# Whole-tile instructions in a split GELU-multiply kernel, with the first and last tiles cut smaller

## The chip, the cores and the metric

The kernel runs on one core of a Trainium2 chip. The metric is device time in microseconds (us) of one execution. The kernel before takes 471.6 us. The names in the profile: ACT is the scalar engine, which computes the GELUs; DVE is the vector engine, which multiplies; SP computes nothing and only issues transfers; the 16 DMA engines move the data.

## The reference

```python
def reference(x):                      # x: (32, 512, 2048) float32
    half_dim = x.shape[-1] // 2
    x1, x2 = x[..., :half_dim], x[..., half_dim:]
    gelu_x1 = 0.5 * x1 * (1 + erf(x1 / np.sqrt(2)))
    return (gelu_x1 * x2).astype(np.float32)
```

134.2 MB come in and 67.1 MB go out, with one GELU and one multiply per output element.

## The kernel before

The 16,384 rows are cut in 16 tiles of 128 partitions x 8 rows. A tile is 8.39 MB of input and 4.19 MB of output. There are two input and two output buffers. Loads are issued from SP's queue and stores from ACT's, except that the last two tiles are stored from SP's.

```python
R, STEP = 8, 4
xpool = ...tile_pool(name="xpool", bufs=2)
opool = ...tile_pool(name="opool", bufs=2)
...
ahead = [load(0), load(1)]                       # nc.sync.dma_start
for i in range(n_tiles):
    x_tile = ahead.pop(0)
    o_tile = opool.tile(...)
    last = i == n_tiles - 1
    for r in range(0, R, STEP):                  # two halves of 4 rows
        rows = slice(r, r + STEP)
        nc.scalar.activation(out=x_tile[:, rows, :half], in_=x_tile[:, rows, :half], func=GELU)
        nc.vector.tensor_mul(out=o_tile[:, rows, :], in0=..., in1=x_tile[:, rows, half:])
        if last:
            store(nc.sync, i, o_tile, rows)
    if not last:
        store(nc.sync if i == n_tiles - 2 else nc.scalar, i, o_tile, slice(0, R))
    if i + 2 < n_tiles:
        ahead.append(load(i + 2))
```

The build, which turns the source into one queue of instructions per engine, orders each queue itself.

## Time and profile before

| | before |
|---|---|
| time, median | 471.6 us |
| profiled span | 469.7 us |
| DVE / ACT busy | 140.2 / 115.2 us |
| moved over the span | 201.3 MB, 429 GB/s |
| period of a tile | 29.0 us at 434 GB/s |

How to read it: compute is busy less than a third of the time (DVE 30%, ACT 25%), and the DMA engines are busy throughout (a share of 1.00 in each stretch of a tile). The prediction below shows the lines. One view that it did not use is the order of ACT's queue. The timeline around tiles 4 and 5 of the kernel before shows it (start, duration, engine, line, operation; in brackets, how long the engine stood idle before and what ended that; ACTq is ACT's sequencer, which issues the DMA):

```profile
131.71 7.12 ACT L54 ACTIVATE x_tile<-x_tile 128x4096 f32<-128x4096 f32 x2 [22.10 <-DMA x_tile<-in_x_dram]
135.36 8.76 DVE L57 TENSOR_TENSOR o_tile<-x_tile 128x4096 f32<-128x4096 f32 x2 [20.47 <-ACT x_tile L54]
144.15 0.36 ACTq L45 DMA_DIRECT2D out_dram<-o_tile  x1
160.50 7.12 ACT L54 ACTIVATE x_tile<-x_tile 128x4096 f32<-128x4096 f32 x2 [21.67 <-DMA x_tile<-in_x_dram]
```

The multiplies of tile 4 end at 144.12 and its store goes out at 144.15, 16.4 us ahead of the next tile's GELU.

### The profile page before, as it was taken

The numbers are of one execution on the slowest core, as the hardware profiler recorded it, in microseconds if no ns is written. First come the engines' busy times: TensorE is split into PE (matmuls) and PEld (weight loads), VectorE is DVE, ScalarE is ACT, GpSimd is POOL, SyncE is SP. The second block draws the span as 40 slices with busy tenths as digits, with TensorE's granted clock in tenths as the row PEclk, the third lists the DMA queues.
The fourth block names the chain that finished last, engine by engine and source line by source line (L and its number), as shares of the span: only waits on it lengthen the run. The fifth ranks groups of instructions, "written<-read, shape, count | busy, mean of one in ns | idle before, by whom it ended". The sixth has DMA issues, their size and how long they took to land.

```text
span 469.7 us, 213 instructions
## 1 busy us (share of the span) xinstructions
DVE 140.2 (30%) x32; ACT 115.2 (25%) x33; POOL 0.2 (0%) x4
## 2 busy tenths in 40 slices
DVE  0070704307042070520606115060250702507043
ACT  1052306023060320603206041060500505005060
POOL 0000000000000000000000000000000000000000
DMA  8999999999999999999999999999999999999988
GB/s 357 446 446 357 446 446 446 402 446 458 391 446 444 433 463 402 435 413 491 402 419 430 491 402 402 446 491 402 402 446 480 413 402 444 449 446 402 474 375 357
DMA packets 4754, 201.35 MB, mean 429 GB/s; under 512 B 528, under 2 KB 528, under 8 KB 528
## 3 DMA queue, kind: packets, MB, share of 16 engines
q1 hardware_dynamic: 2736, 142.61, 70.5%
q10 hardware_dynamic: 2016, 58.72, 29.0%
q14 instruction: 2, 0.02, 0.0%
HBM read 134.22 MB, written 67.11 MB: 429 GB/s over the span
## 4 chain that ended last, share of the span: by engine, by line
DMA 77%; DVE 14%; ACT 6%; DVEq 1%; issue 0%; SPq 0%; ACTq 0%
DMA x_tile<-in_x_dram 77%; DVE o_tile L57 14%; ACT x_tile L54 6%; DVEq L93 1%; SPq L41 0%; ACTq L54 0%
## 5 line engine op out<-in xcount | busy, mean ns | idle before, releaser
L57 DVE TENSOR_TENSOR o_tile<-x_tile 128x4096 f32<-128x4096 f32 x32 | 140.2, 4422 | 321.6 <-ACT x_tile L54 321.6
L54 ACT ACTIVATE x_tile<-x_tile 128x4096 f32<-128x4096 f32 x32 | 114.0, 3608 | 340.5 <-DMA x_tile<-in_x_dram 340.5
L54 ACT ACT_TABLE_LOAD x1 | 1.3, 1283 | 0.7 <-PEq L82 0.7
L82 POOL MEMSET const-bfloat16-1.0<- 128x1 bf16 x1 | 0.1, 102 | 0.0
L82 POOL MEMSET const-uint8-127<- 128x1 uint8 x1 | 0.1, 101 | 0.0
L82 POOL MEMSET const-float32-0.0<- 128x1 f32 x1 | 0.1, 99 | 0.2 <-issue 0.2
L82 POOL MEMSET const-float32-1.0<- 128x1 f32 x1 | 0.1, 98 | 0.0
## 6 DMA issues: line engine op xcount, KB each, us to landing
out_dram<-o_tile ACTq DMA_DIRECT2D x14, 4096.0 KB, 41.8
out_dram<-o_tile SPq DMA_DIRECT2D x1, 4096.0 KB, 24.8
out_dram<-o_tile SPq DMA_DIRECT2D x2, 2048.0 KB, 6.9
x_tile<-in_x_dram SPq DMA_DIRECT2D x16, 45.5
```

What stands on the lines that cost most here:

```text
L54: nc.scalar.activation(out=x_tile[:, rows, :half], in_=x_tile[:, rows, :half], func=GELU)
L57: nc.vector.tensor_mul(out=o_tile[:, rows, :], in0=x_tile[:, rows, :half], in1=x_tile[:, rows, half:],)
L82: nc = _bacc.Bacc("TRN2", target_bir_lowering=False, num_devices=1)
L93: with _tile.TileContext(nc) as tc:
```

## The change

The intent is fewer instructions: one GELU and one multiply for a whole tile. The first tile keeps its two halves. The last is cut in 1, 1, 2 and 4 rows, so that the end of the kernel has less to wait for.

```diff
-    R, STEP = 8, 4
+    R = 8
...
-        for r in range(0, R, STEP):
-            rows = slice(r, r + STEP)
+        if last:
+            steps = (0, 1), (1, 2), (2, 4), (4, 8)
+        else:
+            steps = ((0, 4), (4, 8)) if i == 0 else ((0, 8),)
+        for lo, hi in steps:
+            rows = slice(lo, hi)
...
-            if last:
-                store(nc.sync, i, o_tile, rows)
+            if last and hi % 4 == 0:
+                store(nc.sync, i, o_tile, slice(hi - 4, hi))
```

## The prediction

The prediction's sum came to 0 + 0 - 0.2 us, thus 471.4 us. The 434 GB/s and the packet times are measured. "3.4 us later" in part one: with the measured 7.12 and 8.76 us of a tile's two GELUs and two multiplies it is 3.5 us, an estimate. "2.0 us earlier" and "0.7 us earlier" in part three, where "they" are the multiplies of the two halves: in e1_stores_first, told below, the two halves end 6.13 and 11.78 us after the GELU's start, so 1.95 and 0.63 us earlier than the 8.08 and 12.41 of the kernel before.

> **What bounds the kernel now.** I read the page first, then the chain of waits, then the windows view, then the groups by form, and last the timeline and DMA records around the end. From the page, busy time, the 40 slices and the queues:
>
> ```profile
> DVE 140.2 (30%) x32; ACT 115.2 (25%) x33; POOL 0.2 (0%) x4
> ...
> DMA  8999999999999999999999999999999999999988
> ...
> HBM read 134.22 MB, written 67.11 MB: 429 GB/s over the span
> ```
>
> Neither compute engine is busy a third of the time, while the DMA row is at 9 from the second slice on and drops only in the last two. The page's chain of waits says the same from the other side: 77% of it is waiting for a load.
>
> ```profile
> DMA 77%; DVE 14%; ACT 6%; DVEq 1%; issue 0%; SPq 0%; ACTq 0%
> ```
>
> But 20% of that chain is DVE and ACT, and that is the misleading part. The chain of waits in order of time shows a cycle for each of the two input buffers:
>
> ```profile
> 56.85 45.55 DMA x_tile<-in_x_dram
> ...
> 102.48 3.62 ACT x_tile L54
> 106.11 0.03 issue
> 106.13 8.77 DVE o_tile L57 x2
> ...
> 114.92 45.50 DMA x_tile<-in_x_dram
> ```
>
> A load is issued at 56.85, lands 45.55 us later, one half-tile GELU (3.62) and two half-tile multiplies (8.77) free the buffer, and the next load into it goes out at 114.92: 58.07 us for two tiles, 29.0 per tile. Read naively, anything added between landing and release lengthens this cycle. Whether it does depends on whether the 45.5 us is transfer or queueing. The first load, with nothing before it, is issued at 1.16 and its tile starts at 22.67 in the timeline: 21.5 us. So some 24 of the 45.5 us are waiting behind the other load and beside the stores. The windows view over four stretches of one tile each decides it (columns: DVE, ACT and POOL busy, clock, DMA share, GB/s):
>
> ```profile
> 73.60:102.60 29.00, 8.76 (x2) 7.21 (x3) 0.00 (x0) 1.00 1.00 434
> 102.60:131.60 29.00, 8.76 (x2) 7.01 (x2) 0.00 (x0) 1.00 1.00 434
> 131.60:160.60 29.00, 8.76 (x2) 7.22 (x3) 0.00 (x0) 1.00 1.00 434
> ```
>
> The DMA share is 1.00. A tile is 8.39 MB in and 4.19 MB out, 12.58 MB, and 12.58 MB / 29.0 us is 434 GB/s. The kernel moves bytes all the time, so the period is the transfer time of a tile and the compute chain lies wholly beside it.
>
> [...]the trace's packet records agree, with a 64 KB load packet (2.418 us) and a 32 KB store packet (1.213 us) in turn, 8 of each per engine per tile: 8 x 3.63 = 29.0 us. [...]
>
> ```profile
> L57 DVE TENSOR_TENSOR o_tile<-x_tile 128x4096 f32<-128x4096 f32 x32 | 140.2, 4422 | 321.6 <-ACT x_tile L54 321.6
> L54 ACT ACTIVATE x_tile<-x_tile 128x4096 f32<-128x4096 f32 x32 | 114.0, 3608 | 340.5 <-DMA x_tile<-in_x_dram 340.5
> ```
>
> **The change, part by part.** [...]
>
> Part one, tiles 1 to 14 in whole-tile instructions. Removed: 14 GELUs and 14 multiplies[...]. Both engines idle for two thirds of the time, so this is worth nothing. Moved: the multiply can't start on the first half while GELU does the second. Landing to release goes from 3.62 + 8.77 = 12.4 us[...]: the next load into the buffer, and the store, go out 3.4 us later. Is there room?
> - Loads. Load 4 goes out at 86.0 (the multiplies of tile 2 start at 77.22 and take 8.76), and load 3 in front of it lands at 102.4: a lead of 16.4 us, which becomes 13.0. A load on an idle queue needs 21.5 us where its bytes need 8.39/0.434 = 19.3, so 2.2 us of lead are enough there. Even at the full rate, with no store beside it, load 3 would last 19.3 us from 73.5, to 92.8; load 4 would go out at 89.4.
> - Stores. The first goes out at 35.11 and lands 34.6 us later, at 69.7; the second goes out at 56.85 and lands 41.8 us later, at 98.7, thus 29.0 after the first: it had waited its turn for some 12.8 us. That wait becomes 9.4. By the packet records the first store took 7.1 us from issue to its first packet with loads in front of it; if the next store needs as much, 2.3 us are left.
> - Output buffers. The store of tile 2 (out at 86.0) lands at 127.8 and the multiply of tile 4 starts at 135.36, later still after the change: no wait.
> So the period stays 29.0 us and the difference here is 0; the loads' median time to landing should fall from 45.5 to about 42.1 and the stores' from 41.8 to about 38.4, as queueing is shortened by exactly what compute takes.
>
> Part two, tile 0, is as before: 0.
>
> Part three, the last tile, in 1, 1, 2 and 4 rows. From the GELU's start at 449.37, [...] Before, they ended at 8.08 and 12.41. So the first output half is ready 2.0 us earlier and the second 0.7 us earlier: the last multiply waits for the GELU of its four rows, which is why little is won there. What is on the path to the end? At 449.3 the last load has landed and 4.19 MB of tile 14's store and 4.19 MB of tile 15's are left. 8.39 MB / 434 GB/s = 19.3 us, so the DMA alone needs until 468.6. The last store goes out at 461.8 and takes 6.6, thus landing at 468.4. So the tail is bound by the DMA too. The windows view of the tail looks lower only because 1.2 us of it come after the last landing:
>
> ```profile
> 449.30:469.70 20.40, 8.76 (x2) 7.12 (x2) 0.00 (x0) 1.00 0.90 386
> ```
>
> By the packet records the first half of the last store left the engines idle for 0.2 us each, as it came just after tile 14's store was through; its second half left none. An issue 2.0 us earlier removes these 0.2 us. Sum: 0 + 0 - 0.2 us: 471.6 - 0.2 = 471.4 us.
>
> **Rivals.** (1) The chain is real: two buffers, cycle 58.07 us plus 3.4, for 14 tiles 7 x 3.4 = 24 us, 495 us (5% slower). For it: the chain of waits with its 20% of compute. Against it: DMA share 1.00 in every period, and 16.4 us of lead. (2) The stores miss their turn, since only some 2 us of lead are left by the last count. The loads would then run ahead alone, at the same total rate, and stores would pile up for the end: some us at most if the tail then runs out of overlapping work, 472 to 475 us. Against it: bytes are conserved and the DMA has loads to move meanwhile. (3) The tail is bound by compute and the full 0.7 to 2.0 us are won: 469.6 to 470.9. For it: the chain ends in the last GELU and multiplies. Against it: the 19.3 us above leave no gap of that size. (4) The tail's split is undone by a shift of tile 14's store, 3.4 us later: it goes out at 437.9 instead of 434.51 on the same queue as the last load, which lands at 449.3, so it is still in line: 0.
>
> **Range and chances.** Rival 1 I hold at 1%, rival 3 at 5%, rival 2 at a few per cent, and these last two stay within 2% (9.4 us) anyway. The three times of before run from 471.57 to 472.48, so noise is larger than my effect. I predict 471.4 us, 8 in 10 between 470.9 and 472.0. Chance of over 2% faster 0.003, within 2% 0.987, slower 0.01.
>
> **What would show it.** Right: windows of 29.0 us per tile at DMA share 1.00 and 434 GB/s; [...]loads landing after about 42.1 us, stores after 38.4; the last load landed near 449.3; the last store issued near 461.1 yet landing near 468.3, so its time to landing rises from 6.6 to about 7.2. Wrong: loads still landing after 45.5 us with a longer period (rival 1), a last load that lands early and a longer tail (rival 2), or a last landing nearer 467 (rival 3).

## The result

| | before | changed |
|---|---|---|
| time, median (range, 5 runs) | 471.57 (471.3 to 472.48) | 478.48 (476.97 to 478.78) |
| profiled span | 469.7 | 474.8 |
| DVE / ACT busy | 140.2 / 115.2 | 139.4 / 114.1 |
| GB/s over the span | 429 | 424 |

The ratio is 1.0139, with a 95% interval of 1.0122 to 1.0156. Ratios are the mean time of one kernel's fast runs over that of the other's of the same rounds, so they are not quite the ratio of the medians. The change is slower by 1.4%, within 2% and far outside the predicted range of 470.9 to 472.0. The profiled run is the fastest of the five, so its profile accounts for 474.8 - 469.7 = 5.1 of the 6.9 us.

From the page of the changed kernel, the lines that answer to those of before: busy engines, DMA over the 40 slices, bytes, and the chain of waits by engine.

```profile
DVE 139.4 (29%) x20; ACT 114.1 (24%) x21; POOL 0.2 (0%) x4
...
DMA  8999999999999999999999999999999999999997
...
HBM read 134.22 MB, written 67.11 MB: 424 GB/s over the span
...
DMA 72%; DVE 14%; ACT 12%; ACTq 0%; issue 0%; SPq 0%
```

The DMA row looks as full as before, yet it moved less per us. The windows view of the changed kernel shows when that begins (columns: DVE, ACT and POOL busy, clock, DMA share, GB/s):

```profile
73.60:102.60 29.00, 8.69 (x1) 7.04 (x2) 0.00 (x0) 1.00 1.00 434
102.60:131.60 29.00, 8.69 (x1) 7.02 (x1) 0.00 (x0) 1.00 1.00 434
...
276.60:305.60 29.00, 8.69 (x1) 6.48 (x1) 0.00 (x0) 1.00 1.00 425
305.60:334.60 29.00, 8.69 (x1) 7.03 (x1) 0.00 (x0) 1.00 1.00 427
```

The stretches from 73.6 and 102.6 run exactly as before, with the whole-tile instructions in place. Later stretches have the same share of 1.00, but 425 to 427 GB/s. What happens in between? The timeline of the changed kernel around tiles 4 and 5:

```profile
131.66 7.03 ACT L59 ACTIVATE x_tile<-x_tile 128x8192 f32<-128x8192 f32 x1 [22.04 <-DMA x_tile<-in_x_dram]
138.72 8.69 DVE L62 TENSOR_TENSOR o_tile<-x_tile 128x8192 f32<-128x8192 f32 x1 [20.37 <-ACT x_tile L59]
147.44 27.86 SPq L42 DMA_DIRECT2D x_tile<-in_x_dram  x2
159.20 7.03 ACT L59 ACTIVATE x_tile<-x_tile 128x8192 f32<-128x8192 f32 x1 [20.51 <-DMA x_tile<-in_x_dram]
159.22 16.12 ACTq L46 DMA_DIRECT2D out_dram<-o_tile  x2
```

The multiply of tile 4 ends at 147.41. SP issues the next load at once, at 147.44. The store of tile 4 goes out only at 159.22, 11.8 us later and just behind the GELU of tile 5, which had waited for its own tile to land. (The line merges two issues: the second, tile 5's, follows at about 175.) A listing of both builds' instructions, shortened, says why, and the traces show the same order:

```
before, ACT:  ... Activation x2 | DMACopy | Activation x2 | DMACopy | Activation x2 ...   (for every tile)
changed, ACT: ... Activation (tile 4) | Activation (tile 5) | DMACopy (4) | DMACopy (5) | ...
```

The build has put the stores of tiles 4, 8 and 12 behind the next tile's GELU. Nothing in the source asks for it. The changed kernel's trace shows the other two as well: the GELU of tile 9 starts at 276.05, and the store of tile 8 goes out at 276.13, though the load that the same multiply releases went out at 262.20. For tile 12 these are 394.33, 394.41 and 380.47.

What a late store does to the DMA engines is in the trace's packet records. Each of the 16 engines moves 8 load packets (2.418 us each) and 8 store packets (1.213 us each) per tile in turn. With the store of tile 4 missing, loads 5 and 6 land after 27.79 and 27.78 us instead of 29.00: each has one store packet of 1.21 us fewer beside it. From there on the stores lag. In the kernel before, a tile's worth of store packets ends 3.6 us ahead of the load beside it (156.35 against 159.98). In the changed kernel it ends 3.8 us behind (190.39 against 186.59). Nothing makes this good: in the packet records loads and stores go in turn, and the stores of tiles 4 to 12 end 3.6 to 3.8 us behind the load beside them, each time.

The bytes are the same, so the shift need not cost anything by itself. But the engines lose step, and load packets get slower. Every load ends with one small record per engine, so the spread of these 16 records says how far the engines are apart. Worked out from the records, in us:

| load | before | changed |
|---|---|---|
| 4 | 0.5 | 0.7 |
| 8 | 0.5 | 1.6 |
| 12 | 0.5 | 2.4 |
| 15 (the last) | 0.6 | 4.7 |

After the first 45 us, 1 load packet of the kernel before took over 60 ns longer than 2.418 us; in the changed kernel 233 did. They cluster where one store ends and the next begins, for instance at 219.0 to 223.8, 248.5 to 253.6 and 278.0 to 283.1, where the stores end at 219.6, 249.6 and 279.2. Summed over all packets, an engine is busy for 470.9 us on average instead of 467.1 (3.71 more before rounding), and idle for 3.9 instead of 2.6 (1.34 more, all of it in the last 15 us). 3.71 + 1.34 = 5.05 us, the difference of the profiled spans.

Losing step and slow packets go together. The records carry no engine number, but an engine's packets can be followed, nearly all of them, by their times. After the first 45 us, the load packets of eight engines took about 2.5 to 3.3 us longer in sum than at 2.418 us each, and those engines end load 15 at 448.4 to 448.8; those of the other eight took 4.0 to 5.5 us longer, and these end it at 451.5 to 453.0.

At the end, the output buffers are late too. The waits of the changed kernel (who waited for what: total us, times, longest) have a line that the kernel before doesn't have:

```profile
DVE o_tile L62 <- DMA out_dram<-o_tile: 16.5, 1, 16.5
```

It is the first multiply of the last tile. Its input is ready at 454.52, but the store that frees its output buffer lands only at about 455.8; 16.5 us is all of DVE's idle time before it, of which the store prolonged the last 1.5 us. This wait is not what ends the kernel late. The last multiply still waits for its GELU (0.26 us idle, ended by ACT), and the engine that ends last never runs dry: its last three records of stores come at 463.93, 468.80 and 473.66, 4.87 and 4.86 us apart, which is the time of the eight packets that each half of the last store has on an engine.

### The profile page after: what moved, and what is told of

It reads as the page before. It is cut to its first block, busy times and chain, and to the rows that moved or that the text cites. A ratio compares the mean times of both kernels' runs of the same rounds, so it can differ in the third digit from the quotient of the medians.

```text
span 474.8 us, 188 instructions
## 1 busy us (share of the span) xinstructions
DVE 139.4 (29%) x20; ACT 114.1 (24%) x21; POOL 0.2 (0%) x4
## 4 chain that ended last, share of the span: by engine, by line
DMA 72%; DVE 14%; ACT 12%; ACTq 0%; issue 0%; SPq 0%
DMA x_tile<-in_x_dram 72%; DVE o_tile L62 14%; ACT x_tile L59 12%; ACTq L98 0%; SPq L42 0%; ACTq L59 0%
## 5 line engine op out<-in xcount | busy, mean ns | idle before, releaser
L62 DVE TENSOR_TENSOR o_tile<-x_tile 128x8192 f32<-128x8192 f32 (+3 forms) x20 | 139.4, 6985 | 325.8 <-ACT x_tile L59 309.2
L59 ACT ACTIVATE x_tile<-x_tile 128x8192 f32<-128x8192 f32 (+3 forms) x20 | 112.8, 5661 | 345.9 <-DMA x_tile<-in_x_dram 345.9
## 6 DMA issues: line engine op xcount, KB each, us to landing
out_dram<-o_tile ACTq DMA_DIRECT2D x14, 4096.0 KB, 41.7
x_tile<-in_x_dram SPq DMA_DIRECT2D x16, 43.1
```

Of the source, the lines that this page charges most:

```text
L62: nc.vector.tensor_mul(out=o_tile[:, rows, :], in0=x_tile[:, rows, :half], in1=x_tile[:, rows, half:],)
```

## The experiments

Theory A: the order of ACT's queue is the cause. A late store shifts stores behind loads, the DMA engines lose step from there on, and the loss grows with each tile that follows. Rival B: the later release of buffers by whole-tile instructions is the cause in itself. Rival C: the last tile's four steps are.

### The changed kernel with its stores kept ahead (e1_stores_first)

```diff
+    with tc.issue_after(stored.ins) if stored is not None else nullcontext():
         nc.scalar.activation(out=..., in_=..., func=GELU)
...
+    stored = s if i < n_tiles - 2 else None      # s: the store just issued
```

> The changed kernel, with each store on ACT's queue held ahead of the next tile's GELU (in the changed kernel the build put the stores of tiles 4, 8 and 12 behind it). Theory A, the order of ACT's queue is the cause: 29.0 us per tile throughout at DMA share 1.00, 471.4 us (470.9 to 472), so 7 us less than the changed kernel. Rival B, the 3.4 us between landing and release are the cause by themselves: the time stays near 478.5 us. Rival C, the last tile's four steps are the cause: it stays near 478.5 as well.

Measured: 471.77 us (4 runs, 471.62 to 472.13), ratio to before 1.0007 (0.9992 to 1.0022). The whole loss is gone with nothing but the order of ACT's queue put back. The windows view of this run, and its DMA issues (number, KB each, median us to landing):

```profile
276.60:305.60 29.00, 8.69 (x1) 6.94 (x2) 0.00 (x0) 1.00 1.00 434
305.60:334.60 29.00, 8.69 (x1) 7.17 (x2) 0.00 (x0) 1.00 1.00 434
...
out_dram<-o_tile ACTq DMA_DIRECT2D x14, 4096.0 KB, 38.4
...
x_tile<-in_x_dram SPq DMA_DIRECT2D x16, 42.1
```

The stretches that had 425 and 427 GB/s are back at 434. Loads land after 42.1 us and stores after 38.4, as the prediction said. The engines' spread stays at 0.7 us through load 15, and not one load packet is slow after 45 us. Rivals B and C fall: their parts are all in this run.

### The kernel before with three stores late (e2_three_late), and with one (e3_one_late)

```diff
+LATE = (4, 8, 12)                               # second kernel: (4,)
...
-            nc.scalar.activation(
+            g = nc.scalar.activation(
...
+            if r == R - STEP and held is not None:
+                with tc.issue_after(g.ins):
+                    store(nc.scalar, *held)
+                held = None
...
-        if not last:
+        if i in LATE:
+            held = (i, o_tile, slice(0, R))
+        elif not last:
```

> The kernel before with its half-tile instructions, and only the stores of tiles 4, 8 and 12 put behind the next tile's GELU. Theory A: 476 to 480 us, stores 4, 8 and 12 issued some 17 us later than they could be, slow load packets from tile 5 on. Rival B or C: 471.6 us, as the DMA is full in any case.

> As the last, but the store of tile 4 alone is late. If one late store shifts stores against loads for good and the shift costs on every later tile: 29.4 to 29.7 us per tile from tile 6 on and 475 to 478 us, nearly as much as three. If each late store costs by itself and the rest recovers: a third of the loss of three late stores, about 473.5 us. Rival B or C: 471.6 us.

Measured: 477.26 us (476.26 to 478.18, ratio 1.012) and 477.27 us (475.22 to 478.09, ratio 1.0116), both with the half-tile instructions of the kernel before. The profile of three late stores has 199 slow load packets after 45 us and a spread of 6.0 us at load 15. So the order alone brings the loss into the old kernel, and the first late store brings all of it.

The profiled run of one late store, the fastest of its four at 475.22, shows the loss on one engine. Only 12 load packets are slow after 45 us, and the engines are busy for 467.4 us on average, but one engine has fallen out of step: at load 15 it ends 5.8 us after the first and 5.1 after the next slowest. Followed by their times, the 12 slow packets are all on that engine (2.5 us in sum), so the form is that of the changed kernel, on one engine instead of all. The last load has landed at 452.03, with that engine, and the last tile's GELU starts at 452.11, so its compute waits for that one engine while the others run dry; it ends at 472.32 and the rest by 471.05. The timeline and the windows view of this run at the end:

```profile
452.11 7.12 ACT L56 ACTIVATE x_tile<-x_tile 128x4096 f32<-128x4096 f32 x2 [22.46 <-DMA x_tile<-in_x_dram]
455.76 8.76 DVE L63 TENSOR_TENSOR o_tile<-x_tile 128x4096 f32<-128x4096 f32 x2 [20.76 <-ACT x_tile L56]
460.21 4.67 SPq L46 DMA_DIRECT2D out_dram<-o_tile  x2
...
457.20:462.20 5.00, 5.00 (x2) 2.03 (x1) 0.00 (x0) 1.00 0.39 165
```

The first half of the last store goes out at 460.21, and in the 5 us around it the DMA share is 0.39. In this run that engine was 3.0 us off from load 1 on, as chance had it. Until the store was late that stayed constant, with loads 29.0 us apart. Not all of this profile's 3.7 us of extra span need come from the late store, then; the reading rests on the times of all four runs, of which the other three took 477.1 to 478.1. Loads 7 to 13 then came 29.1 to 29.3 us apart, less than the 29.4 to 29.7 that was expected, and the last two 29.7. (A rerun of the same kernel need not show the same engine or form.)

### Late at the end, and late at the start (e5_late_12, e6_late_1)

The edit is that of the last kernel with `LATE = (12,)` and `LATE = (1,)`.

> The kernel before with only the store of tile 12 behind the next tile's GELU. If the loss builds up tile by tile after the shift (the spread of the 16 DMA engines' landing times grew by some 0.4 us a tile in the changed kernel's trace): 3 tiles instead of 11 are left, so 472.5 to 474 us. If each late store costs its loss at once, or in the tail alone: 476 to 478 us, as with the store of tile 4.

> As the last, but the store of tile 1 alone is late. If the loss builds up tile by tile, 14 tiles instead of 11 are left: 477 to 480 us, at least what the late store of tile 4 cost. If it is a fixed cost: 476 to 478 us again. If the order of the queues only matters late in the kernel: 471.6 us.

Measured: 471.96 us with tile 12 late (ratio 1.0003, 0.999 to 1.0017) and 479.65 us with tile 1 late (1.0172, 1.0154 to 1.0189). The first is somewhat below what was expected, the second within it. With tile 4 at 477.27 between them, the loss grows with the number of tiles that follow: about (479.65 - 471.96) / 11 = 0.7 us per tile. It isn't a fee for the event. The profile of tile 1 late shows the same within one run: from load 4 on, each load comes 29.3 to 29.9 us after the one before, instead of 29.0.

### Late, then caught up (e8_late_then_caught_up, e9_late_loads_only)

If the lag of the stores is what costs, letting them catch up must stop the loss. On top of the kernel with tile 4 late, the loads of tiles 8 and 9 were held back a little, each by a GELU of one column that waits for the tile before and is overwritten by the load. The control has the held loads and no late store.

```diff
+LATE_LOADS = (8, 9)
...
+        if after is not None:     # after: the input of the tile before
+            nc.scalar.activation(out=x_tile[:, 0, 0:1], in_=after[:, 0, half:half + 1], func=GELU)
         nc.sync.dma_start(out=x_tile, in_=x_t[i])
...
+        if i + 1 in LATE_LOADS:
+            ahead.append(load(i + 1, x_tile))
```

> The kernel before with the store of tile 4 late (as in the run that had only that, 477.3 us), and then the loads of tiles 8 and 9 held back by some 3 us each, by a one-column GELU that waits for the tile before to land, so that the stores catch up on the loads by about two packets. If the shift of stores behind loads is what costs on each tile: from tile 10 on 29.0 us a tile and a spread of the DMA engines that no longer grows, 473 to 475 us. If the late store set off something that the phase does not undo (engines once out of step stay so and drift on): 477 us or more.

> The control of the last: the two loads held back and no late store. Stores then run ahead by about two packets. If only a lag of the stores costs: 471.5 to 473 us. If any change of phase costs: 475 to 478 us.

Measured: 473.77 us (472.8 to 477.16, ratio 1.0063) and 472.85 us for the control (471.75 to 473.43, ratio 1.0025). The windows view of the caught-up run, ahead of the held loads, beside them and after:

```profile
189.60:218.60 29.00, 8.76 (x2) 6.24 (x4) 0.00 (x0) 1.00 1.01 431
247.60:276.60 29.00, 8.76 (x2) 7.22 (x3) 0.00 (x0) 1.00 1.01 427
...
305.60:334.60 29.00, 8.76 (x2) 7.12 (x2) 0.00 (x0) 1.00 1.00 434
334.60:363.60 29.00, 8.76 (x2) 7.12 (x2) 0.00 (x0) 1.00 1.00 434
```

From load 10 to load 14 each load lands exactly 29.00 us after the one before. The engines' spread was 0.9 us at load 5, grew to 3.3 by load 9, and stays at 3.3 through load 14. (The hold did more than was meant: the store of tile 9 ends 12.8 us ahead of the load beside it, where the kernel before has 3.6.) So in this run the engines, once 3.3 us apart, didn't drift on by themselves: between these two queues it was the lag of the stores that drove them. The loss already made isn't given back, and the held loads cost 1.5 us by themselves, going by the control. One of the four runs took 477.16 (the interval of the ratio is 1.0017 to 1.0109), so catching up didn't work equally well each time.

### All DMA on one queue (e7_one_queue)

```diff
-            store(nc.sync if i == n_tiles - 2 else nc.scalar, i, o_tile, slice(0, R))
+            store(nc.sync, i, o_tile, slice(0, R))
```

> The changed kernel with all stores on SP's queue, each just ahead of the load that its tile releases, so that one queue holds everything in a fixed order and ACT's order can't delay a store. If two queues whose shares can shift against one another, and engines that then lose step, are the cause: no engine spread that grows (below 1 us), no slow load packets at the first store, 469.5 to 471.5 us, thus at best 1 to 2 us below the kernel before. If the whole-tile instructions or their later release cost by themselves: 475 us or more. A rival that speaks against the single queue: loads and stores no longer overlap[...]: 480 us or more.

Measured: 475.43 us (6 runs, 474.85 to 476.35), ratio 1.0079 (1.0065 to 1.0092). A miss: ACT's order can't delay a store here, and yet it is slower than the kernel before. By its own expectation 475 us or more would speak for a cost of the whole-tile instructions, but these cost nothing in e1_stores_first (471.77 us, 3.7 less), so that reading falls. Its spread grows too, from 0.7 us at the first load to 4.4 at the last, in steps that fall on the loads and not on the stores. Why it grows here is not shown. So losing step isn't particular to two queues. What two queues in the right phase have is that they don't lose it (0.7 us through load 15 in e1_stores_first). This was the attempt at a version better than both kernels, and it isn't one. The changed kernel with its order put back equals the kernel before with fewer instructions.

### The last tile (e4_tail_only, e10_last_whole)

The first is the kernel before with only its last tile in 1, 1, 2 and 4 rows; the second is the changed kernel with the order put back and its last tile in one step (`steps = ((0, 8),)` and one store).

> The kernel before with only its last tile cut in 1, 1, 2 and 4 rows. Theory A: 471.4 us, 0.2 less than before, within the noise: the gap of 0.2 us before the first half of the last store goes, and the last landing moves by no more. Rival C: some us slower than before, towards 478.

> The changed kernel with the stores kept ahead of the GELUs (471.8 us) and its last tile in one step too. By the sums for the tail: the last store goes out at 449.0 + 7.0 + 8.7 = 464.8 us and has 4.19 MB = 9.7 us to move plus some 1.5 us of latency, so it lands near 476 instead of 468: 479 us (478 to 480). If the split of the last tile is worth nothing: 471.8 us.

Measured: 471.47 us (ratio 1.0002, 0.9987 to 1.0017) and 478.7 us (ratio 1.0153). Both as expected. (The 1.5 us of latency in the second expectation is an estimate; the last store of the kernel before landed 6.6 us after its issue, and its eight packets on an engine, 0.614 us each, are 4.9 of them, so 1.7 us are left.) Cutting the last tile at all is worth 7 us (478.7 against 471.8). Cutting it finer than in two halves is worth nothing that the runs can show (471.47 against 471.57), as each DMA engine has some 19.5 us of stores to move after the last load in any case (8 packets of 1.213 us and 16 of 0.614, by the records of the kernel before).

## Why the prediction was wrong

**Right.** The kernel is bound by the DMA engines (a share of 1.00, with DVE busy 30% and ACT 25%). The change of durations is worth nothing: with whole-tile GELUs of 7.03 us and multiplies of 8.69, e1_stores_first took 471.77 us. DVE fell only from 140.2 to 139.4 us, as two half-tile multiplies already overlapped (8.76 us for the pair, where 2 x 4.42 = 8.84). The sums for slack held (loads at 42.1 and stores at 38.4 us to landing in the run with the order put back; 43.1 and 41.7 in the changed kernel itself), and so did the period of 29.0. The last tile's chain came out as forecast: the last multiply of that run ends 456.35 + 4.43 - 449.00 = 11.78 us after the GELU's start, 0.63 us earlier than before, against 0.7. That run took 471.8 us, inside the range.

**The step that failed** is in part one: "the next load into the buffer, and the store, go out 3.4 us later", and from it "So the period stays 29.0 us and the difference here is 0". For three of the 14 whole tiles the store didn't go out when the multiply ended, but only with the next tile's GELU, 11.8 us later still for tile 4, 13.9 for tile 8 and 14.0 for tile 12. I had taken the order of ACT's queue as given, and the build chose another for the changed kernel. The queue's order could have been listed among the risks, because stores and GELUs share it.

**Rival 2** had the mechanism's first half: "The stores miss their turn", loads run ahead alone, stores pile up for the end. It was held at a few per cent for another reason, too little lead, and that did not happen. Its size was off as well. That "bytes are conserved" is true, but the rate isn't: the lagging stores made the 16 engines lose step and slowed load packets, and that was most of the 5 us. The prediction saw the DMA as one pipe of 434 GB/s, and it is 16 engines, of which the slowest decided when a tile had landed: load 15 of the changed kernel was through on the first at 448.4 us and on the last at 453.0, and its GELU started at 453.46. The last load therefore came late (at 453.0 us by the packet records, 448.9 before) and not early, as rival 2 would have had it.

**What stays open.** Why lagging stores slow load packets (233 in the changed kernel), when leading ones hardly do (1 in the kernel before), no run here shows. The packets say where it happens (where one store ends and the next begins) and not why. How many engines the slow packets fall on also varies: one in the profile of one late store, all 16 in that of the changed kernel, though eight of them lost more than the rest.

## What to carry to other kernels

When a change alters the instructions, compare the order of each engine's instructions before and after, above all on an engine that both computes and issues transfers: here the store of tile 4 stood behind a GELU that waited for its load, and went out 11.8 us late. In a kernel bound by DMA, a share of 1.00 doesn't say that all is well: here equal stretches moved 425 to 427 GB/s instead of 434 at that share, and the DMA engines ended the last load 4.7 us apart instead of 0.6. Look at both. A small shift between two steady streams can stay and cost a little on every later tile: in the changed kernel the stores stayed some 3.6 us behind, and one late store cost about 0.7 us for each tile that followed (e5_late_12 against e6_late_1).
